# Norms spread over the update matmuls, four first units, a later convolution, and adaLN steps on ACT and POOL

## The chip, the cores and the metric

The kernel runs on one core of a Trainium2 chip. The time is that of one launch on the device, in microseconds (us); the lower the better. The engines are named as in the profile: PE does the matrix products and PEld loads their weights, DVE is the vector engine, ACT the activation engine, POOL the GpSimd engine, and SP starts most of the transfers (DMAs). Each engine works through its own list of instructions in order; it waits on semaphores for the others.

## The reference

The input is one sequence of 1024 tokens with 1024 channels and one conditioning vector c. Two layers follow each other; each has a mixer and a feed-forward part (ConvFFN), and each of these four blocks begins with a norm and ends with a gated addition to x. Cut to what matters here:

```
cs = silu(c)
for i in (0, 1):
    mod = cs @ ada_w[i] + ada_b[i]                 # (6 * 1024): the adaLN vector
    sh_m, sc_m, g_m, sh_f, sc_f, g_f = split(mod, 6)
    hm = rms_norm(x, norm_mix[i]) * (1 + sc_m) + sh_m
    y = even_mixer(hm) if i == 0 else odd_mixer(hm)
    x = x + g_m * y
    hf = rms_norm(x, norm_ffn[i]) * (1 + sc_f) + sh_f
    x = x + g_f * conv_ffn(hf)

conv_ffn(h): gate, val = split(h @ w_up, 2)        # 1024 -> 2 * 2816
    gate = causal_dwconv(gate, conv_w) + conv_b    # three taps over the tokens
    return (silu(gate) * val) @ w_down             # 2816 -> 1024
```

The even mixer is a gated delta rule beside windowed pooling, the odd one is dilated window attention with three groups of heads. All is float32.

## The kernel before

**Layout.** x lives as eight tiles `xt[k]` of 128 channels by 1024 tokens. Tokens are worked in two halves of 512 (`HS`). Every product is done three times (`mm3`, L203 to L208): each operand is split into a high part `hi` (rounded to the fast format) and a low part `lo` (the rest), and hi times hi, hi times lo and lo times hi are added up in PSUM. `split` (L182) makes a pair: ACT copies the high part (L183), another engine, POOL as a rule, subtracts it (L184). Weights come as granules of 128x512 numbers: a DMA into a `raw` tile (four of them in rotation), then `split` into `whi` and `wlo` (nine of each in rotation).

**PSUM.** There are two tiles `mm` (1024 columns) and four tiles `sp` (512 columns), each a rotation: who asks for the next one waits until the last reader of the oldest has finished.

**Order of the work.** The program is written as generators. A dense generator issues matmuls and yields the time of each step (`3 * MM`, 0.648 for an `mm3`); `weave` (L92) runs a chain of other work between them: where the chain yields a number, the dense generator is stepped until its yields add up to that number. When the kernel is built, a planner fixes the order of each engine's list from this text order and its own estimates of when each instruction is ready, so that a later instruction may stand ahead of an earlier one that is not yet ready. On the chip the lists run strictly in order.

**The edges.** Where one block ends and the next begins, the last four row blocks of the output product are added to x by half: `edge` (L423) issues the eight channel tiles of the first half, then `edge_end` (L417) weaves the norm of the first half into the matmuls of the second. Each finished tile is added to x by DVE (L240), squared by ACT (L343, L346), and the squares are summed by DVE (L347). `norm` (L384) sums over the channels with four PE transposes and a DVE reduction (L307, L308), takes the reciprocal root in twelve small DVE steps (`rsqrt`), spreads it into an `sp` tile by PE (L354), and then `normed` (L379) does for each of the eight tiles: DVE multiplies by the root, read from PSUM (L367), ACT applies scale and shift (L374), DVE makes the high part (L376), and the low part is subtracted by POOL for even tiles and by DVE for odd ones (L377). All eight tiles are issued in one go. There are three such edges: from the even mixer to its ConvFFN (about 530 us), from that ConvFFN to the odd mixer (about 1245 us), from the odd mixer to its ConvFFN (about 2365 us).

**The first units of ConvFFN.** `first_two` (L1138) computes the channel blocks 0 and 1 of gate and value. While the second half of h is not there, it runs three units over the first half (gate 0, value 0, gate 1), with the norm of the second half woven in; then gate 0, value 0 and gate 1 over the second half, and value 1 over both halves in a third `mm` tile. `conv_half` (L1109) does the convolution of one half out of PSUM: ACT the centre tap (L1102), DVE the others (L1098); `act` (L1119) applies silu and multiplies by the value. `h_sums` (L1172) and `w_sums` (L1227) then form sums of the blocks of h and of the weights, and the blocks 2 to 21 run as seven products each (`up`, L1232).

**The down stage.** For the 22 hidden blocks two at a time (a pair), `update` (L220) takes four granules and two hidden blocks (split into `oh` by ACT and `ol` by POOL, 128x1024 each), and does 16 units of two `mm3`; DVE adds each `sp` tile to x (L240).

**The adaLN steps.** The adaLN vector of the two layers is not computed at once: `ada_steps` (L260) does it in sections of 512 numbers with eight steps each. A step loads 128x512 weights into a `raw` tile and DVE multiplies them by a column of cs and adds them to `ada_acc` (L274 the first, L276 the others); after eight, PE and DVE sum over the partitions (`ada_cols`, L307, L308, L321). `step_back` (L109) issues one step at every second unit of the down stage of layer 0 (`pace[0] = 2`, L1274). The very first sections are done by `ada_pair` (L283), which can do a step on ACT and POOL: ACT scales the raw tile in place (L293), POOL adds it to the sum (L295).

## Time and profile before

| | us |
|---|---|
| median of 3 runs (lowest, highest) | 3082.81 (3079.80, 3086.07) |
| the profiled execution | 3081.34 |
| its span, first to last instruction | 3079.6 |

| engine | busy us | share of the span |
|---|---|---|
| PE | 2967.4 | 96% |
| DVE | 2018.0 | 66% |
| ACT | 1074.1 | 35% |
| POOL | 972.2 | 32% |

The span is the time from the first to the last instruction of the profiled execution; the launch has 1.7 us more. A busy share is an average over stages that differ; below, views of single stretches are shown, and the times in them are counted from the start of the span. `<-` after a wait names what ended it. PE is counted busy while a matmul's records say so; matmuls follow each other closer than their own durations, so that their spacing says more than their durations.

### The profile page before, as it was taken

Reading aid. Unit: us, or ns where it says so; the run is one execution under the profiler, and the core shown is the slowest. Engines: PE = TensorE matmul, PEld = TensorE weight load, DVE = VectorE, ACT = ScalarE, POOL = GpSimd, SP = SyncE. Lnnn points to the kernel's source line nnn. Section 1 sums busy time; section 2 is a strip of 40 time slices with the busy share of each in tenths; the row PEclk is TensorE's granted clock in tenths of the full one; section 3 lists DMA queues with packets and bytes.
Section 4 is the critical chain, followed back from the end, with each engine's and each line's share of the span. In section 5 each row is a group of like instructions: output and inputs, shape, how many; then the busy total and the mean of one; then the engine's idle time right before and its main releaser. Section 6 shows DMA issues by size and latency. Waiting matters only on the chain.

```text
span 3079.6 us, 40200 instructions
## 1 busy us (share of the span) xinstructions
PE 2967.4 (96%) x14346; PEld 2446.9 (79%) x14346; DVE 2018.0 (66%) x3877; ACT 1074.1 (35%) x2170; POOL 972.2 (32%) x727
## 2 busy tenths in 40 slices
PE   6999999899999899999999999999999899999999
PEld 4777878678888777788888878888877788888888
DVE  7877745987777877754445646354687877776554
ACT  4434422433333211323333333324343433333210
POOL 4412323555555543200000010000022655555540
PEclk8999999999999999999999999999999999999999
DMA  7523323253323753221313242313243222224321
GB/s 248 145 63 99 96 91 121 72 158 110 110 86 106 240 164 114 106 86 61 106 61 114 65 149 72 115 37 117 68 163 114 85 89 83 82 82 168 110 90 59
DMA packets 275010, 331.46 MB, mean 108 GB/s; under 512 B 27411, under 2 KB 194426, under 8 KB 274810
## 3 DMA queue, kind: packets, MB, share of 16 engines
q1 hardware_dynamic: 266810, 300.55, 31.0%
q0 software_dynamic: 7040, 25.17, 2.4%
q10 hardware_dynamic: 960, 3.18, 0.3%
q8 instruction: 113, 1.85, 0.2%
q14 instruction: 87, 0.71, 0.1%
HBM read 251.82 MB, written 77.00 MB: 107 GB/s over the span
## 4 chain that ended last, share of the span: by engine, by line
PE 72%; DVE 7%; DMA 3%; issue 2%; POOL 1%; ACT 1%; SPq 0%; POOLq 0%; DVEq 0%; ACTq 0%
PE sp L206 11%; PE sp L207 11%; PE sp L208 11%; PE mm L1356 8%; PE mm L1354 8%; PE mm L1355 8%; PE mm L206 3%; PE mm L207 3%; PE mm L208 3%; PE sp L1550 2%; PE sp L1506 2%; PE sp L1386 1%; DVE ada_acc L276 1%; PE sp L1539 1%; DMA raw<-in_ada_w_dram 1%
## 5 line engine op out<-in xcount | busy, mean ns | idle before, releaser
L1354 PE MATMUL mm<-whi,hh 128*128 128x512 f32 x1152 | 482.7, 419 | 0.0
L1356 PE MATMUL mm<-whi,hl 128*128 128x512 f32 x1152 | 452.7, 393 | 0.0
L1355 PE MATMUL mm<-wlo,hh 128*128 128x512 f32 x1152 | 451.6, 392 | 0.0
L184 POOL TENSOR_TENSOR wlo<-raw,whi 128x512 fp32r<-128x512 f32 x190 | 257.0, 1367 | 544.5 <-ACT whi L183 463.8
L183 ACT ACTIVATE whi<-raw 128x512 fp32r<-128x512 f32 x334 | 208.4, 630 | 389.6 <-PE sp L207 163.0
L240 DVE SCALAR_TENSOR_TENSOR xr<-sp,mod,xr 128x512 f32<-128x512 f32 x336 | 248.0, 747 | 135.6 <-PE sp L208 135.2
L206 PE MATMUL sp<-oh,whi 128*128 128x512 f32 (+1 forms) x832 | 315.6, 379 | 20.2 <-DVE xr L240 14.2
L207 PE MATMUL sp<-ol,whi 128*128 128x512 f32 (+1 forms) x832 | 311.1, 374 | 0.0
L208 PE MATMUL sp<-oh,wlo 128*128 128x512 f32 (+1 forms) x832 | 311.0, 374 | 0.0
L206 PE MATMUL mm<-hh,whi 128*128 128x512 f32 x736 | 299.6, 407 | 8.8 <-DVE ft L1098 6.8
L207 PE MATMUL mm<-hl,whi 128*128 128x512 f32 x736 | 294.0, 399 | 3.2 <-POOL hl L377 1.6
L208 PE MATMUL mm<-hh,wlo 128*128 128x512 f32 x736 | 293.1, 398 | 0.0
L184 POOL TENSOR_TENSOR wlo<-t2k,whi 128x512 fp32r<-128x512 f32 x160 | 228.8, 1443 | 159.0 <-ACT whi L183 120.7
L1451 POOL DMA_DIRECT2D vd<-v x24 | 17.6, 735 | 771.9 <-ACT v L1448 379.4
L1356 PEld LDWEIGHTS mm<-whi,hl 128*128 128x128 f32 x1152 | 216.6, 188 | 48.0
L1355 PEld LDWEIGHTS mm<-wlo,hh 128*128 128x128 f32 x1152 | 217.9, 189 | 37.2 <-DVE wlo L184 0.2
L1354 PEld LDWEIGHTS mm<-whi,hh 128*128 128x128 f32 x1152 | 217.5, 189 | 36.1
L184 POOL TENSOR_TENSOR wlo<-wr,whi 128x512 fp32r<-128x512 f32 x114 | 177.5, 1559 | 161.5 <-ACT whi L183 158.6
L206 PEld LDWEIGHTS sp<-oh,whi 128*128 128x128 f32 x832 | 157.0, 189 | 55.7 <-DVE xr L240 21.6
L208 PEld LDWEIGHTS sp<-oh,wlo 128*128 128x128 f32 x832 | 157.1, 189 | 28.2
L207 PEld LDWEIGHTS sp<-ol,whi 128*128 128x128 f32 x832 | 157.1, 189 | 26.3
L206 PEld LDWEIGHTS mm<-hh,whi 128*128 128x128 f32 x736 | 140.8, 191 | 38.8 <-issue 10.7
(395 smaller groups left out, 6147.4 us busy)
## 6 DMA issues: line engine op xcount, KB each, us to landing
raw<-in_ada_w_dram SPq DMA_DIRECT2D x160, 256.0 KB
wr<-in_ffn_w_up_dram SPq DMA_DIRECT2D x76, 512.0 KB
raw<-in_od_w_in_dram SPq DMA_DIRECT2D x144, 256.0 KB
hid<-ft SPq DMA_DIRECT2D x44, 512.0 KB
raw<-in_ffn_w_down_dram SPq DMA_DIRECT2D x88, 256.0 KB
big<-hid SPq DMA_DIRECT2D x44, 512.0 KB
xr<-xs SPq DMA_DIRECT2D x32, 512.0 KB
os<-stg SPq DMA_DIRECT2D x96, 130.0 KB
```

The source lines that it names most:

```text
L183: nc.scalar.activation(dst_hi, src, AF.Copy)
L184: eng.tensor_tensor(out=dst_lo, in0=src, in1=dst_hi, op=ALU.subtract)
L206: nc.tensor.matmul(ps, wh, mh, start=first, stop=False)
L207: nc.tensor.matmul(ps, wh, ml, start=False, stop=False)
L208: nc.tensor.matmul(ps, wl, mh, start=False, stop=last)
L240: nc.vector.scalar_tensor_tensor(out=xt[o][:, s], in0=p, scalar=gate[:, o:o + 1], in1=xt[o][:, s], op0=ALU.mult, op1=ALU.add)
L276: nc.vector.scalar_tensor_tensor(out=acc, in0=raw, scalar=cs[:, k:k + 1], in1=acc, op0=ALU.mult, op1=ALU.add)
L1354: nc.tensor.matmul(p, hh, wh, start=(k == 0), stop=False)
L1355: nc.tensor.matmul(p, hh, wl, start=False, stop=False)
L1356: nc.tensor.matmul(p, hl, wh, start=False, stop=(k == KT - 1))
L1506: nc.tensor.matmul(ps[:, at:at + len(ks) * P], qks[i][0][:, hh, blk * P:(blk + 1) * P], qks[i][1][:, hh, ks[0] * P:(blk + 1) * P], start=T ...
L1550: nc.tensor.matmul(ps[:, j * P:(j + 1) * P], pTs[n][:, a0 + c * P:a0 + (c + 1) * P], vb(kb, hh), start=(c == 0), stop=(c == len(ks) - 1))
```

## The change

The change has four parts.

1. In `norm`, the eight tiles are issued one at a time, with a yield of `apart` after each. `edge_end` sets `apart` to 1.3, so that steps of the update's second half stand between the tiles; the other callers leave it at zero. In `moved`, the high part of odd tiles is now made by ACT, straight from the tile before its scale and shift, ahead of the scale and shift in place; for even tiles DVE makes it as before.
2. In `first_two`, four units run over the first half (value 1 is the fourth, in an `sp` tile), and value 1 over the second half goes to a second `sp` tile; the third `mm` tile is no longer asked for. The second wait of the norm of the second half is 6.0 and no longer 5.5.
3. The convolution of the first half of gate 0 is issued after the matmuls of its second half, beside that of the second half.
4. From the down stage of layer 0 on, the adaLN steps run as in `ada_pair` on ACT and POOL: ACT scales the raw tile by the column of cs (in place, or into `ada_acc` for the first step), POOL adds it for the other seven.

```diff
--- before.py
+++ after.py
@@ -104,6 +104,7 @@
 
     pa = [None]
     back = []
+    by_pool = [False]
     beat, pace, secs_done, secs_due = [0], [3], [0], [12]
 
     def step_back(now=False):
@@ -270,7 +271,11 @@
             yield 1
             for k in range(KT):
                 nxt = load(s, k + 1) if k < KT - 1 else None
-                if k == 0:
+                if by_pool[0]:
+                    nc.scalar.activation(raw if k else acc, raw, AF.Copy, scale=cs[:, k:k + 1])
+                    if k:
+                        nc.gpsimd.tensor_tensor(out=acc, in0=acc, in1=raw, op=ALU.add)
+                elif k == 0:
                     nc.vector.tensor_scalar(out=acc, in0=raw, scalar1=cs[:, 0:1], scalar2=None, op0=ALU.mult)
                 else:
                     nc.vector.scalar_tensor_tensor(out=acc, in0=raw, scalar=cs[:, k:k + 1], in1=acc,
@@ -371,9 +376,12 @@
 
         a, b = vec
         s = HS[hf]
+        hh, hl = h[k]
+        if k % 2:
+            nc.scalar.activation(hh[:, s], t, AF.Identity, scale=a[:, k:k + 1], bias=b[:, k:k + 1])
         nc.scalar.activation(t, t, AF.Identity, scale=a[:, k:k + 1], bias=b[:, k:k + 1])
-        hh, hl = h[k]
-        nc.vector.tensor_copy(hh[:, s], t)
+        if not k % 2:
+            nc.vector.tensor_copy(hh[:, s], t)
         (nc.vector if k % 2 else nc.gpsimd).tensor_tensor(out=hl[:, s], in0=t, in1=hh[:, s], op=ALU.subtract)
 
     def normed(xt, vec, h, hf, rstd, ks=range(KT), keep=False):
@@ -381,11 +389,12 @@
         for k in ks:
             moved(scaled(xt, k, hf, rstd, keep), vec, h, k, hf)
 
-    def norm(xt, vec, h, hf, acc, wait=(2.5, 5.8), keep=False):
+    def norm(xt, vec, h, hf, acc, wait=(2.5, 5.8), keep=False, apart=0.0):
         yield wait[0]
         rstd = yield from rstd_row(acc[hf], wait[1])
-        normed(xt, vec, h, hf, rstd, keep=keep)
-        yield 1.2
+        for k in range(KT):
+            normed(xt, vec, h, hf, rstd, (k,), keep)
+            yield apart
 
     osp = dram.tile([8, P, T], F32, name="osp")
     osp2 = dram.tile([4, P, T], F32, name="osp2")
@@ -416,7 +425,7 @@
 
     def edge_end(acc, tl, xt, vec, h, keep=None):
 
-        weave(norm(xt, vec, h, 0, acc, keep=keep is not None), tl)
+        weave(norm(xt, vec, h, 0, acc, keep=keep is not None, apart=1.3), tl)
         drain(tl)
         return acc
 
@@ -1138,25 +1147,25 @@
             def first_two():
 
                 gp, vp = mm_ps(), mm_ps()
-                g = [[gp[:, s] for s in HS], [s_ps(), None]]
-                wb = [wu_gate(0), wu_val(0), wu_gate(1)]
+                g, v = ([[p[:, s] for s in HS], [s_ps(), None]] for p in (gp, vp))
+                wb = [wu_gate(0), wu_val(0), wu_gate(1), wu_val(1)]
                 t = [gate_tile(), gate_tile()]
-                d = units([gp, vp, g[1]], wb, h, (0,))
-                weave(norm(xt, vec, h, 1, acc, (4.5, 5.5), keep=True), d)
+                d = units([gp, vp, g[1], v[1]], wb, h, (0,))
+                weave(norm(xt, vec, h, 1, acc, (4.5, 6.0), keep=True), d)
                 drain(d)
-                conv_half(t[0], g[0], 0, 0)
                 drain(units([gp], wb[:1], h, (1,)))
-                conv_half(t[0], g[0], 0, 1)
+                for hf in range(2):
+                    conv_half(t[0], g[0], 0, hf)
                 conv_half(t[1], g[1], 1, 0)
                 drain(units([vp], wb[1:2], h, (1,)))
-                act(t[0], [vp[:, s] for s in HS], 0)
+                act(t[0], v[0], 0)
                 sums = h_sums()
                 g[1][1] = s_ps()
-                drain(units([[None, g[1][1]]], wb[2:], h, (1,)))
+                drain(units([[None, g[1][1]]], wb[2:3], h, (1,)))
                 conv_half(t[1], g[1], 1, 1)
-                vp = mm_ps()
-                drain(units([vp], [wu_val(1)], h))
-                act(t[1], [vp[:, s] for s in HS], 1)
+                v[1][1] = s_ps()
+                drain(units([[None, v[1][1]]], wb[3:], h, (1,)))
+                act(t[1], v[1], 1)
                 return sums
 
 
@@ -1271,7 +1280,7 @@
                 up(j, b, a)
                 a = nxt
             xt = reload(xs[2 + l])
-            pace[0] = 2
+            pace[0], by_pool[0] = 2, True
             for j in range(0, NJ - 4, 2):
                 if j:
                     hid = [from_dram(hid_d[l][i]) for i in (j, j + 1)]
```

## Rows read from the trace of the kernel before

**Rows 1.** Busy time by engine in stretches of 100 us: stretch, its length, then busy us (and instructions) of PE, PEld, DVE, ACT and POOL, the granted PE clock as a share of full speed, the DMA share and GB/s.
```profile
500.00:600.00 100.00, 89.63 (x392) 71.67 (x390) 75.71 (x123) 34.33 (x53) 41.78 (x27) 0.98 0.26 84
1000.00:1100.00 100.00, 90.70 (x386) 71.37 (x385) 80.09 (x100) 25.03 (x32) 51.41 (x29) 0.98 0.67 222
...
2900.00:3000.00 100.00, 100.00 (x443) 82.81 (x442) 55.21 (x74) 21.04 (x28) 44.19 (x27) 1.00 0.28 90
```

**Rows 2.** What PE waited for from 1000 to 1320 us (the down stage of layer 0 and the edge behind it): the PE instruction, what ended its wait, us in total, times, longest us.
```profile
PE sp L206 <- DVE xr L240: 14.2, 16, 2.4
PE sp L354 <- DVE rs L131: 1.2, 1, 1.2
PE sp L307 <- DVE t2k L347: 1.2, 1, 1.2
PE sp L206 <- DVE t2k L367: 1.1, 1, 1.1
```

**Rows 3.** The same from 500 to 640 us (the edge from the even mixer to its ConvFFN, and the first units).
```profile
PE mm L206 <- DVE ft L1098: 3.4, 1, 3.4
PE sp L206 <- DVE xr L367: 2.5, 1, 2.5
PE sp L307 <- DVE t2k L347: 2.1, 1, 2.1
PE sp L354 <- DVE rs L131: 1.3, 1, 1.3
PE mm L207 <- POOL hl L377: 0.9, 1, 0.9
PE mm L207 <- DVE hl L377: 0.8, 1, 0.8
```

**Rows 4.** PE's instructions in order of time at the edge from the odd mixer to its ConvFFN, those with a wait of over 2 us before them: start, us, line, operation, and in brackets the idle time before it and what ended it.
```profile
2382.98 0.47 PE L206 MATMUL sp<-oh,whi 128*128 128x512 f32 x1 [2.46 <-DVE xr L367]
...
2394.22 0.66 PE L307 MATMUL sp<-ident,t2k 128*128 128x128 f32 x4 [2.11 <-DVE t2k L347]
...
2432.85 0.71 PE L206 MATMUL mm<-hh,whi 128*128 128x512 f32 x1 [3.41 <-DVE ft L1098]
```

**Rows 5.** DVE's groups of instructions from 538.8 to 561.6 us, from the first tile of the norm of the first half to the last sum of squares of the second: line, operation, count, busy us, mean ns of one, idle us before them.
```profile
L376 DVE CAST hh<-xr 128x512 fp32r<-128x512 f32 x8 | 6.4, 794 | 0.0
L347 DVE TENSOR_TENSOR t2k<-t2k,t2k 128x512 f32<-128x512 f32 x6 | 6.0, 1002 | 0.2
L367 DVE TENSOR_TENSOR xr<-xr,sp 128x512 f32<-128x512 f32 x8 | 5.3, 676 | 0.8 <-PE sp L354 0.8
L240 DVE SCALAR_TENSOR_TENSOR xr<-sp,mod,xr 128x512 f32<-128x512 f32 x5 | 3.6, 738 | 0.0
L377 DVE TENSOR_TENSOR hl<-xr,hh 128x512 fp32r<-128x512 f32 x4 | 3.2, 804 | 0.0
```

**Rows 6.** ACT's groups in the same stretch.
```profile
L374 ACT ACTIVATE xr<-xr,mod,nA 128x512 f32<-128x512 f32 x8 | 6.4, 811 | 3.9 <-DVE xr L367 3.9
L183 ACT ACTIVATE whi<-raw 128x512 fp32r<-128x512 f32 x7 | 4.2, 621 | 0.4 <-issue 0.4
L346 ACT ACTIVATE t2k<-xr 128x512 f32<-128x512 f32 x6 | 3.7, 630 | 2.6 <-DVE xr L240 2.5
```

**Rows 7.** DVE's instructions in order of time, at two places: columns as in rows 4.
```profile
558.32 3.20 DVE L347 TENSOR_TENSOR t2k<-t2k,t2k 128x512 f32<-128x512 f32 x2
565.93 0.69 DVE L1227 TENSOR_TENSOR t2k<-raw,raw 128x512 f32<-128x512 f32 x1 [4.41 <-DMA raw<-in_ffn_w_up_dram]
566.54 0.68 DVE L308 TENSOR_REDUCE rs<-sp 128x4 f32<-128x512 f32 x1
...
1037.50 0.82 DVE L274 TENSOR_SCALAR ada_acc<-raw,cs 128x512 f32<-128x512 f32 x1
```

**Rows 8.** PE's instructions in order of time, at two places: the first and last of seven matmuls after the wait that ended at 561.58 us, the first after them, and the transposes of an adaLN section.
```profile
562.65 0.63 PE L206 MATMUL sp<-hh,whi 128*128 128x512 f32 x1
...
565.21 0.63 PE L206 MATMUL mm<-hh,whi 128*128 128x512 f32 x1
...
566.19 0.40 PE L206 MATMUL sp<-hh,whi 128*128 128x512 f32 x1
...
1063.02 0.60 PE L307 MATMUL sp<-ident,ada_acc 128*128 128x128 f32 x4
```

**Rows 9.** Groups of instructions from 1020 to 1215 us, the down stage of layer 0 (columns as in rows 5).
```profile
L240 DVE SCALAR_TENSOR_TENSOR xr<-sp,mod,xr 128x512 f32<-128x512 f32 x130 | 94.3, 744 | 25.7 <-PE sp L208 25.4
L276 DVE SCALAR_TENSOR_TENSOR ada_acc<-raw,cs,ada_acc 128x512 f32<-128x512 f32 x48 | 57.8, 1205 | 12.5 <-DMA raw<-in_ada_w_dram 12.3
L184 POOL TENSOR_TENSOR wlo<-raw,whi 128x512 fp32r<-128x512 f32 x36 | 49.2, 1379 | 48.0 <-ACT whi L183 35.2 <-PE sp L208 6.4 <-PE sp L207 6.3
...
L184 POOL TENSOR_TENSOR ol<-big,oh 128x1024 fp32r<-128x1024 f32 x18 | 44.7, 2487 | 51.3 <-PE sp L207 29.7 <-ACT oh L183 19.7 <-PE sp L208 1.9
```

**Rows 10.** One of POOL's groups from 0 to 110 us, where `ada_pair` does its steps on ACT and POOL (columns as in rows 5).
```profile
L295 POOL TENSOR_TENSOR ada_acc<-ada_acc,whi 128x512 f32<-128x512 f32 x3 | 4.2, 1397 | 2.7 <-ACT whi L293 2.6
```

**Rows 11.** Who waited for whom from 1015 to 1215 us, all engines: three of the rows (columns as in rows 2).
```profile
ACT whi L183 <- PE sp L207: 52.0, 8, 10.1
...
POOL ol L184 <- PE sp L207: 29.7, 5, 8.4
...
DVE ada_acc L276 <- DMA raw<-in_ada_w_dram: 13.7, 8, 3.2
```

## The prediction

> **What bounds the kernel now.** I read the busy time in stretches of 100 us first [rows 1]. From 2900 to 3000 us PE runs 443 instructions in 100 us and never idles: there the matmuls alone set the time, 0.226 us each and 0.68 for an `mm3`. The stretches that the change touches fall short of that, 392 instructions from 500 us and 386 from 1000 us, with DVE at 76 and 80 us of 100. So the kernel is bound by PE, and time is to be won only where PE waits. The waits say where that is, and each of them names DVE or what DVE feeds. In the down stage of layer 0 it is 14.2 us in 16 waits for the gated addition L240, which frees an `sp` tile [rows 2]. At the edge into layer 0's ConvFFN it is 3.4 + 2.5 + 2.1 + 1.3 + 0.9 + 0.8 = 11.0 us [rows 3], at the same edge of layer 1 three of these come again with the same length [rows 4], and I take the edges as equal, and at the edge between the layers 1.2 + 1.2 + 1.1 = 3.5 us [rows 2]. A wait costs more than itself: behind the one that ended at 561.58 us, PE was at the lower of its two levels, seven matmuls from 562.65 us spaced by (565.21 - 562.65) / 6 = 0.43 us, which is 512 columns at 1.2 GHz, against 0.23 us after 566.19 us [rows 8]. That is 7 x 0.2 = 1.4 us, and I take as much behind the 3.4 us wait: 2.6 us of clock for an edge. All in all 14.2 + 2 (clock) + 2 x 13.6 + 3.5 = 47 us can be won at most, as far as these rows reach.
>
> **Part 4, the down stage.** Why is L240 late? It takes 744 ns each time, so nothing slows it; but in DVE's list it stands behind L276, 48 steps of a mean 1205 ns with 12.5 us of idle before them for the weights' DMA [rows 9]. A step has the form of L240 but reads both inputs from SBUF, as POOL's subtractions do; L240 reads one from PSUM, and keeps its 744 ns beside a POOL that is busy half the time. I read the 0.46 us that a step takes longer as time lost against POOL, and take it that more work on POOL will not lengthen L240.
>
> With the change DVE keeps L240 alone, 94 us of 200. All 14.2 us of waits and the clock behind the first, 2 us, go, and bounds are 0 and 16 us by these rows. The work goes to ACT, 54 scalings of about 0.63 us (the nearest row is a square of the same size, 630 ns [rows 6]) = 34 us on an engine with 25 us busy of 100 [rows 1], and to POOL, 48 additions of 1.40 us, the row of the same addition at the start [rows 10], = 67 us. POOL has 49.2 + 44.7 = 94 us already [rows 9], so 161 us of some 183 us: 88%, the fullest engine after PE. What it delays is `wlo` and `ol`, which stand behind additions that wait for ACT, and ACT for the DMA (13.7 us for DVE now [rows 11]). The cover is their lead: ACT waits 52.0 us and POOL 29.7 us for PE to give tiles back [rows 11], so they are done about a pair ahead, and PE waits for neither in the whole stage [rows 2]. The transposes of an adaLN section sit in PE's list too; those at 1063.02 us [rows 8] belong to a section whose eight steps were over when the next began at 1037.50 us [rows 7], 25 us earlier, so POOL may be that late. The cover is thin only in the first two pairs, where hidden blocks and weights come in while the steps start. There I leave 2 us, and take a gain of 14 us.
>
> **Parts 1 to 3, an edge into a ConvFFN.** I go along the waits.
>
> The 2.5 us: PE wants an `sp` tile while the root's tile is held by all eight multiplications (L367) and the additions L240 stand behind them. Tile by tile, 1.3 lets pass three `mm3` (0.648 each, two are short of it), so the additions stand between the tiles. The root's tile stays held longer, until the last tile, but three others rotate at 12 x 0.226 = 2.7 us each. This wait goes; the work behind it does not. From 538.8 to 561.6 us DVE never idles, but for 1.0 us at its start [rows 5]. Of its 22.8 us the change takes four of the eight casts, 6.4 / 2 = 3.2 us, which leaves 19.6. From the same start PE has 19 `mm3` of the update and 7 before the transposes, 26 x 0.68 = 17.7 us. So the transposes still wait about 2 us (now 2.5 + 2.1). ACT gets four more, 4 x 0.81, and one more granule: 14.3 + 3.2 + 0.6 = 18.1 us [rows 6], also beside 17.7, so it is no cover for DVE but not behind it. Bounds of this remainder: 0 and 4.6 us.
>
> The 1.3 us: the reduction L308 stands behind a sum of weights L1227 that waited 4.41 us for its DMA [rows 7]. The raw tiles of value 1 now stand ahead of those sums in the rotation, so this DMA starts later in the text's order, while the update that frees `whi` ends earlier. The wait of the root has one `mm3` more of cover (10 for 6.0, 9 for 5.5). I take 0.7 us, bounds 0 and 4.4.
>
> The 0.9 + 0.8 us for `hl` of the second half: a fourth unit of 8 x 0.68 = 5.4 us stands before the first use, against a lack of under a microsecond each. Gone.
>
> The 3.4 us: value 1 waited for the `mm` tile of gate 0, which frees after the convolution L1098. With two `sp` tiles that question is gone, and the later convolution is covered by the four units of the second half, 21.8 us. What is late next: all four `sp` tiles are then held by gate 1 and value 1, and block 2's second product needs one, which frees after the convolution of gate 1, behind the same DVE work. Bounds 0 and 3.4; I take 1.0.
>
> New: the fourth unit needs two more granules in the first round, and the nine `whi` are held by the update until its end; 0 to 1.5 us by ACT's 0.62 and POOL's 1.4 for one [rows 6, 9], taken 0.7. For the clock I leave 0.7 of 2.6.
>
> Sum of what stays: 2 + 0.7 + 1.0 + 0.7 + 0.7 = 5.1 of 13.6, a gain of 8.5 us, twice: 17. The edge between the layers has no first units; there the same casts go and the 1.1 us wait for a tile, and I take 2 of 3.5.
>
> **Sum.** 14 + 17 + 2 = 33 us. The profiled execution took 3081.3 us (span 3079.6 and 1.7 around it), so 3048.3; the median of the runs is 1.5 us above that execution, which gives 3049.8. I say 3049.
>
> **Rivals.** First, the edges only move their waits: DVE and ACT have 19.6 and 18.1 us of work for 17.7 us of PE, and every handoff from ACT to DVE within a tile can stall both lists. For it speaks that PE's waits at the edges are all for DVE's chain; against it, that 3.4 + 1.7 us of them hang on tiles and order that the change alters. Then only the down stage gains: 3082.8 - 14 - 1 = 3068.
>
> Second, the down stage gains nothing, because the four raw tiles are now held for DMA, ACT and POOL in a row, and the steps and the granules share them. Against it speaks the lead of a pair. Then 3082.8 - 19 = 3064.
>
> Third, slower: POOL becomes the bound of the down stage. Per pair it has 4 x 1.379 + 2 x 2.487 = 10.5 us and 48 / 9 = 5.3 additions. PE needs 22.2 us a pair (96 matmuls of 0.226 and the transposes), so up to (22.2 - 10.5) / 5.3 = 2.2 us for an addition, its waiting in POOL's list included, nothing happens. The kernel is slower by 6 us, the edges' gains included, when nine pairs take 14.2 + 2 + 19 + 6 = 41 us beyond PE's need, 4.6 each: 3.1 us an addition, 1.7 of it waiting. Then 3089 and more. DVE's steps waited 13.7 / 48 = 0.3 us each on the DMA [rows 11], so I hold it unlikely. The Trainium skill, GPSIMD Engine Reference, section "4.1 Engine selection", speaks for this rival: it gives elementwise additions to VectorE and calls GPSIMD about twice as slow; 1397 against 744 ns agrees, and by the rule alone 48 x 0.65 = 31 us of engine time are lost, which on the path, beside the edges' gain, would give 3081.3 + 31 - 19 = 3093.
>
> Fourth, no effect: the planner's order makes new waits of the size of those that go, say a root delayed by 4.4 us or more at each edge and the slow first pairs; then within 6 us of 3082.8.
>
> **Chances.** The forecast, 3038 to 3060: 0.60. All waits gone, 3030 to 3037: 0.04. Edges only moved: 0.13. Down stage without gain: 0.11. No effect: 0.05. Slower: 0.07. A measurement of this kernel tells about 0.2%, 6.2 us, from no change. So faster 0.88, the same 0.05, slower 0.07. The range takes in the two half gains: 3032 to 3070; the forecast's own is 3038 to 3060.
>
> **What would show it.** In the down stage, PE's waits for L240 are gone, DVE is at some 94 us of 200, POOL near 160, and PE waits neither for `wlo`, `ol` nor for the transposes of a section; waits for POOL there would prove the third rival. At the edges, no wait for L367 and none for `hl`, none for an `mm` tile behind L1098, and one of about 2 us for L347. If that one is 4 us or more, the first rival is right. A DMA wait ahead of L308 longer than 4.4 us would show the order wrong. More than 6 us at the start of block 2 would break the fourth term of the edge.

## The result, and the profile after

The changed kernel takes 3064.0 us (median of 6 runs, 3061.65 to 3069.38), the kernel before 3085.0 beside it: a ratio of 0.9935 [0.9922, 0.9948]. On the 3082.8 us of the prediction that is 20 us less, where 33 were forecast; the range of 3032 to 3070 holds it. The profiled execution had a span of 3067.3 us, the longest of the six.

Both traces have 14346 matmuls, and PE runs them in nearly the same order. So the start of the k-th matmul can be set beside that of the same matmul before, and the offset tells where time is won and lost (worked out from the traces' PE records; the last column is from a second trace of the changed kernel, which is told of under the experiments):

| k-th matmul | starts before (us) | offset after (us) | what lies since the row above | gained (-) or lost | the same, second trace |
|---|---|---|---|---|---|
| 200 | 74.4 | +3.1 | start and first norm | +3.1 | +4.2 |
| 2400 | 504.4 | +3.1 | even mixer | 0.0 | -1.9 |
| 3000 | 657.8 | +0.6 | edge into ConvFFN 0 | -2.5 | -2.4 |
| 5400 | 1218.4 | -20.6 | up stage and down stage | -21.2 | -21.1 |
| 5700 | 1287.7 | -14.0 | end of the down stage, edge between the layers | +6.6 | +5.2 |
| 11000 | 2351.5 | -12.8 | odd mixer | +1.2 | -2.4 |
| 11500 | 2478.3 | -12.2 | edge into ConvFFN 1 | +0.6 | 0.0 |
| 14346 | 3074.8 | -12.2 | ConvFFN 1 | 0.0 | 0.0 |

Nearly all that is won is won in the down stage, a quarter to a third of that is lost right behind it, the two edges into a ConvFFN give 1.9 and 2.4 us together, and the start loses 2 to 4. In the mixers, which the change leaves alone, the two traces of one kernel differ by 1.9 and 3.6 us. So a row is read only where several traces agree on it.

Even the 2.5 us of the first edge are not the edit's. Up to matmul 2960, at 645 us, the changed kernel has lost 0.6 us there. What it wins, 3.1 us from #2960 to #3000, lies behind the end of [rows 3], at a wait that is 2.05 us in the kernel before and 0.6 in the changed one:

```profile
650.26 0.47 PE L206 MATMUL sp<-t,whi 128*128 128x512 f32 x1 [2.05 <-DVE ft L1244]
```

A kernel whose edge is that of the kernel before (part 4 alone, below) has only 0.4 us of this wait and wins 3.2 us there too.

The busy time of the changed kernel by stretches of 100 us (columns as in [rows 1]):

```profile
1000.00:1100.00 100.00, 100.00 (x449) 82.80 (x448) 60.46 (x83) 43.23 (x58) 77.05 (x51) 1.00 0.66 209
1100.00:1200.00 100.00, 100.00 (x452) 82.45 (x450) 61.71 (x82) 38.11 (x54) 74.57 (x51) 1.00 0.53 158
1200.00:1300.00 100.00, 94.07 (x407) 75.32 (x406) 58.58 (x112) 44.00 (x65) 24.67 (x24) 0.97 0.35 118
```

Up to 1200 us the down stage now looks like the stretch that PE alone bounds: 100.00 us busy, 449 matmuls where [rows 1] had 386. The next 100 us fall back to 94 and a granted clock of 0.97. The groups of the changed kernel from 1000 to 1200 us (columns as in [rows 9]):

```profile
L241 DVE SCALAR_TENSOR_TENSOR xr<-sp,mod,xr 128x512 f32<-128x512 f32 x144 | 107.4, 750 | 77.6 <-PE sp L209 77.6
...
L277 POOL TENSOR_TENSOR ada_acc<-ada_acc,raw 128x512 f32<-128x512 f32 x49 | 63.6, 1299 | 20.0 <-ACT ada_acc L275 12.0 <-ACT raw L275 6.1 <-POOL ada_acc L277 0.2
L185 POOL TENSOR_TENSOR ol<-big,oh 128x1024 fp32r<-128x1024 f32 x20 | 48.0, 2401 | 12.7 <-ACT oh L184 12.5
L185 POOL TENSOR_TENSOR wlo<-raw,whi 128x512 fp32r<-128x512 f32 x33 | 42.2, 1293 | 17.0 <-ACT whi L184 17.0
```

This answers to [rows 9]: L241 (L240 before) keeps its length, 750 against 744 ns, and what it waits for is PE, 77.6 us. POOL has 63.6 + 48.0 + 42.2 = 153.8 of 200 us, and its idle time was spent waiting for ACT. PE's waits at the places of [rows 2 to 4], one fence each. From 1000 to 1320 us (columns as in [rows 2]):

```profile
PE sp L209 <- POOL wlo L185: 1.9, 2, 1.2
PE sp L207 <- ACT whi L184: 1.6, 2, 1.0
PE sp L312 <- DVE t2k L352: 1.1, 1, 1.1
PE sp L359 <- DVE rs L132: 1.1, 1, 1.1
```

From 500 to 640 us, the first edge, all that PE waited for:

```profile
PE sp L207 <- DVE ft L1107: 6.5, 1, 6.5
PE sp L209 <- POOL wlo L185: 2.5, 1, 2.5
PE sp L207 <- ACT whi L184: 1.7, 1, 1.7
```

From 2300 to 2480 us, the third edge:

```profile
PE sp L207 <- DVE ft L1107: 3.7, 1, 3.7
...
PE sp L209 <- POOL wlo L185: 2.5, 1, 2.5
PE sp L207 <- DVE ft L1253: 2.3, 1, 2.3
PE sp L207 <- ACT whi L184: 1.6, 1, 1.6
```

The 16 waits for L240 are gone, and so are all six of [rows 3]. At the first edge 10.7 us of others stand in the place of 11.0: the granules of the first round (`whi`, `wlo`: 4.2) and an `sp` tile that the convolution L1107 (L1098 before) gives back late (6.5).

### The profile page after: what moved, and what is told of

The parts are those of the page before. It is cut to its first block, busy times and chain, and to the rows that moved or that the text cites. A ratio compares the mean times of both kernels' runs of the same rounds, so it can differ in the third digit from the quotient of the medians.

```text
span 3067.3 us, 40298 instructions
## 1 busy us (share of the span) xinstructions
PE 2965.9 (97%) x14346; PEld 2452.8 (80%) x14346; DVE 1945.1 (63%) x3781; ACT 1138.9 (37%) x2266; POOL 1033.0 (34%) x783
## 4 chain that ended last, share of the span: by engine, by line
PE 73%; DVE 6%; POOL 2%; issue 2%; DMA 2%; ACT 1%; SPq 0%; POOLq 0%; ACTq 0%; DVEq 0%
PE sp L209 11%; PE sp L207 11%; PE sp L208 11%; PE mm L1365 8%; PE mm L1363 8%; PE mm L1364 8%; PE mm L208 3%; PE mm L207 3%; PE mm L209 3%; PE sp L1559 2%; PE sp L1515 2%; PE sp L1395 1%; DVE xr L1181 1%; PE sp L1548 1%; POOL wlo L185 1%
## 5 line engine op out<-in xcount | busy, mean ns | idle before, releaser
L185 POOL TENSOR_TENSOR wlo<-raw,whi 128x512 fp32r<-128x512 f32 x190 | 250.0, 1331 | 492.6 <-ACT whi L184 425.0
L241 DVE SCALAR_TENSOR_TENSOR xr<-sp,mod,xr 128x512 f32<-128x512 f32 x336 | 251.1, 749 | 183.5 <-PE sp L209 183.5
L207 PE MATMUL mm<-hh,whi 128*128 128x512 f32 x704 | 285.3, 405 | 1.7 <-DVE big L609 1.7
L208 PE MATMUL mm<-hl,whi 128*128 128x512 f32 x704 | 280.0, 398 | 2.2 <-DVE hl L385 2.2
L209 PE MATMUL mm<-hh,wlo 128*128 128x512 f32 x704 | 279.8, 397 | 0.0
L207 PE MATMUL sp<-hh,whi 128*128 128x512 f32 x384 | 152.3, 396 | 13.5 <-DVE ft L1107 10.2
```

Source lines behind the costliest of these rows:

```text
L185: eng.tensor_tensor(out=dst_lo, in0=src, in1=dst_hi, op=ALU.subtract)
L207: nc.tensor.matmul(ps, wh, mh, start=first, stop=False)
L208: nc.tensor.matmul(ps, wh, ml, start=False, stop=False)
L209: nc.tensor.matmul(ps, wl, mh, start=False, stop=last)
L241: nc.vector.scalar_tensor_tensor(out=xt[o][:, s], in0=p, scalar=gate[:, o:o + 1], in1=xt[o][:, s], op0=ALU.mult, op1=ALU.add)
```

## The experiments

Twelve kernels ran. They come from the changed kernel by the edits shown, but for the first, which comes from the kernel before.

**Which part pays.** Part 4 alone, on the kernel before:

```diff
+                if by_pool[0]:
+                    nc.scalar.activation(raw if k else acc, raw, AF.Copy, scale=cs[:, k:k + 1])
+                    if k:
+                        nc.gpsimd.tensor_tensor(out=acc, in0=acc, in1=raw, op=ALU.add)
...
-            pace[0] = 2
+            pace[0], by_pool[0] = 2, True
```

> The kernel before with part 4 alone. Theory: part 4 wins some 21 us in the down stage and gives 6 to 7 back right behind it, where the last eight weight granules wait behind adaLN tiles in the rotation of four; so about 15 us faster than before, ratio 0.995, and PE waits for whi and wlo in the last update although the edge is the old one. Rival: that loss belongs to the new norm at the edge (ACT's copies, spread tiles); then this kernel has no such waits and is 20 us or more faster, ratio 0.9935 or less.

Measured: 0.9955 [0.994, 0.997]. That is what was expected. By the k-th matmul it wins 21.0 us from #3000 to #5400 and loses 7.8 from there to #5700, as the whole change does, with waits of 2.3 us for `wlo` and 1.4 for `whi` beside the old edge. The loss belongs to part 4. All but part 4:

```diff
-            pace[0], by_pool[0] = 2, True
+            pace[0] = 2
```

> The changed kernel without part 4, so parts 1 to 3 alone. Theory: they are worth next to nothing together (some 2.5 us won at the first edge, 0 at the third, 2 to 3 lost at the start, where the same function makes the first h): ratio 0.998 to 1.001, with PE waiting at each edge into a ConvFFN about 4 us for the fourth unit's granules and 4 to 6.5 us for an sp tile at block 2. Rival: parts 1 to 3 bring 6 us or more (ratio 0.998 or less), and the rest of what the changed kernel lacks was lost by part 4.

Measured: 0.9976 [0.9964, 0.9988]; the down stage is as before (0.0 us, and 14.5 us of waits for L241 are back), nothing is lost behind it, and edge 2 wins 1.7. Parts 1 to 3 are worth about 0.24%, 7 us [4, 11] (2.8 by the last matmul of the profiled execution), not 19. So the ratio agrees with the rival (6 us or more) and the trace with the theory, and the interval leaves both; that the loss is part 4's holds either way. The two ratios give 0.45 + 0.24 = 0.69% together, and the change 0.65%: as far as the intervals tell, the parts add up and neither hides the other.

**What is lost behind the down stage.** SP's list of the changed kernel near the end of the stage (start, us from the first issue to the last, line, transfer, count):

```profile
1170.47 22.84 SPq L265 DMA_DIRECT2D raw<-in_ada_w_dram  x11
1194.37 10.04 SPq L189 DMA_DIRECT2D raw<-in_ffn_w_down_dram  x8
```

Eleven adaLN tiles go through the four raw tiles before the last eight granules of `w_down` may: what is left of the steps is issued ahead of the last block (`sections(24)`, L1292). They take 22.84 us, and the granules start at 1194. The same order, no faster, stands in the kernel before:

```profile
1166.55 23.45 SPq L264 DMA_DIRECT2D raw<-in_ada_w_dram  x11
1191.03 10.72 SPq L188 DMA_DIRECT2D raw<-in_ffn_w_down_dram  x8
```

So the eleven loads are not slower with ACT and POOL than they were with DVE; why they take that long in both is not shown here. What has changed is when PE asks: the matmul that waits first, at 1202.88 us in the changed kernel, began at 1221.39 before, and the last granules are issued 2.7 us later than they were. The loads did not follow when PE won 21 us, and a delay that the waits for L240 had covered came out. PE's instructions there, those with a wait, and two of those behind them (columns as in [rows 4]):

```profile
1202.88 0.50 PE L209 MATMUL sp<-oh,wlo 128*128 128x512 f32 x1 [1.22 <-POOL wlo L185]
...
1203.92 0.50 PE L207 MATMUL sp<-oh,whi 128*128 128x512 f32 x1 [0.54 <-ACT whi L184]
...
1205.34 0.50 PE L209 MATMUL sp<-oh,wlo 128*128 128x512 f32 x1 [0.69 <-POOL wlo L185]
...
1206.88 0.80 PE L207 MATMUL sp<-oh,whi 128*128 128x512 f32 x1 [1.04 <-ACT whi L184]
...
1208.82 0.63 PE L207 MATMUL sp<-oh,whi 128*128 128x512 f32 x1
1209.25 0.63 PE L208 MATMUL sp<-ol,whi 128*128 128x512 f32 x1
```

The waits are 3.5 us; behind them the spacing is 1209.25 - 1208.82 = 0.43 us, the lower of the two levels of the clock. Two cures that have nothing in common tell whether it is the shared rotation: the steps of the stage in tiles of their own,

```diff
-                back.append(ada_steps(1, range(0, 48, 4), raw_tile))
+                back.append(ada_steps(1, range(0, 48, 4), lambda: t2k() if by_pool[0] else raw_tile()))
```

> The changed kernel, with the adaLN weights of the down stage loaded into the t2k rotation of eight (idle there) and no longer into the raw rotation of four that the granules use. Theory: the 6 to 8 us lost right behind the down stage come from the last eight granules, which wait for raw tiles behind eleven adaLN tiles; with tiles of their own PE has no whi or wlo wait there and the kernel is 6 us faster than the changed one, ratio about 0.9915. Rival: POOL or ACT themselves are late (161 us of work in 183); then the granules come as late as before, within 1.5 us of the changed kernel.

and more steps in the up stage, so that fewer are left for the down stage:

```diff
-                secs_due[0], pace[0] = 24, 14
+                secs_due[0], pace[0] = 24, 10
```

> The changed kernel with a step every 10 products, not every 14, in the up stage of layer 0, so that some 16 of the steps run there on DVE and the down stage has fewer. Theory: the steps end before the last granules are due; the 6 to 8 us behind the down stage go, the up stage stays bound by PE (DVE at 75 us of 100): ratio about 0.9915. Rival: the up stage's DVE has no room and the up stage grows by what the edge wins; within 2 us of the changed kernel.

Measured: 0.9913 [0.9895, 0.9931] and 0.9902 [0.9887, 0.9917]. Both theories hold. From #5400 to #5700 they win 1.7 and 1.3 us on the kernel before, where the changed kernel loses 6.6. The gain from #3000 to #5400 is 21.7 us with pace 10 and 18.5 with tiles of their own: there PE waits 2.4 us for POOL's `ol` once, at 1018 us, in the first pairs, which no kernel with the shared rotation does. (Their ratios hold more than this: they also win 7.3 and 7.0 us at the first edge, which the cures don't touch; the last section has the reason.) SP's list with tiles of their own:

```profile
1159.08 20.33 SPq L189 DMA_DIRECT2D raw<-in_ffn_w_down_dram  x8
```

The last granules of `w_down` are issued by 1159.08 + 20.33 = 1179.4 us and not by 1194.37 + 10.04 = 1204.4. With pace 10, all of PE's waits from 1000 to 1290 us:

```profile
PE sp L312 <- DVE t2k L352: 1.1, 1, 1.1
PE sp L359 <- DVE rs L132: 1.1, 1, 1.1
```

No `whi` and no `wlo`. The loss of 8 us (6.6 + 1.7, or 1.3) comes from the adaLN loads that stand ahead of the last granules in the one rotation.

**The edges.** Part 2 undone, parts 1, 3 and 4 kept:

```diff
-                wb = [wu_gate(0), wu_val(0), wu_gate(1), wu_val(1)]
+                wb = [wu_gate(0), wu_val(0), wu_gate(1)]
...
-                d = units([gp, vp, g[1], v[1]], wb, h, (0,))
-                weave(norm(xt, vec, h, 1, acc, (4.5, 6.0), keep=True), d)
+                d = units([gp, vp, g[1]], wb, h, (0,))
+                weave(norm(xt, vec, h, 1, acc, (4.5, 5.5), keep=True), d)
...
-                v[1][1] = s_ps()
-                drain(units([[None, v[1][1]]], wb[3:], h, (1,)))
-                act(t[1], v[1], 1)
+                vp = mm_ps()
+                drain(units([vp], [wu_val(1)], h))
+                act(t[1], [vp[:, s] for s in HS], 1)
```

> The changed kernel with three first units again (part 2 undone; parts 1, 3 and 4 kept). Theory: the fourth unit costs more than it covers: without it the granule waits of 1.7 + 2.5 us and the sp wait of 6.5 and 3.7 us go from both edges, the 3.4 us wait for an mm tile comes back, and the kernel is 5 to 10 us faster than the changed one, ratio about 0.991 to the one before. Rival: the sp wait is DVE's backlog and only changes its name; then the mm wait is as long as the sp wait was (4 to 6 us), and the kernel is within 3 us of the changed one.

Measured: 0.9925 [0.991, 0.994], 3 to 4 us faster than the changed kernel by ratio and median, which lies between the theory and the rival and inside both intervals; the profiled third edge wins 7.1 us where the changed kernel loses 0.6 (the first: 3.6 and 2.5). The granules' waits and that for the `sp` tile are gone. PE's waits of this kernel from 500 to 640 us:

```profile
PE mm L208 <- DVE hl L385: 3.0, 3, 1.2
PE sp L312 <- DVE t2k L352: 3.0, 1, 3.0
PE mm L207 <- DVE ft L1132: 2.3, 1, 2.3
PE sp L359 <- DVE rs L132: 1.5, 1, 1.5
PE mm L207 <- DVE ft L1107: 0.3, 1, 0.3
```

10.1 us of waits again: against [rows 3] the one for L1107 (3.4 before) is 0.3, with part 3 in place, those for L352 and `hl` are longer, and one of 2.3 us for the `mm` tile that L1132 frees is new. The casts back on DVE, everything else as changed:

```diff
-        if k % 2:
-            nc.scalar.activation(hh[:, s], t, AF.Identity, scale=a[:, k:k + 1], bias=b[:, k:k + 1])
         nc.scalar.activation(t, t, AF.Identity, scale=a[:, k:k + 1], bias=b[:, k:k + 1])
-        if not k % 2:
-            nc.vector.tensor_copy(hh[:, s], t)
+        nc.vector.tensor_copy(hh[:, s], t)
```

> The changed kernel with all high parts made by DVE again (that half of part 1 undone). Theory: the 2.2 us wait for hl near 66 us of the span and with it 2 to 3 us at the start go, and at the edges DVE has 3.2 us more and ACT 3.2 us less work each, so that the granule waits (ACT's splits come earlier) shrink while the waits for DVE grow: within 3 us of the changed kernel. Rival: ACT's copies relieve the edges; then this kernel is 5 us or more slower than the changed one.

Measured: 0.993 [0.9915, 0.9945], within 3 us of the changed kernel, as expected. At the edges the copies on ACT mostly move the waits: with all casts on DVE, PE waits 3.1 us for L352 again, and 1.1 for the granules in place of 4.2. At the start they cost 2.9 us (+0.2 against +3.1 at #200): `moved` also serves the first norm, where ACT is what PE's first products wait for. ACT in the changed kernel there, and the wait that comes of it, which the kernel before does not have:

```profile
62.35 1.53 ACT L382 ACTIVATE t2k<-t2k,mod,nA 128x512 f32<-128x512 f32 x2 [4.19 <-DVE nA L549]
63.78 0.80 ACT L381 ACTIVATE hh<-t2k,mod,nA 128x512 fp32r<-128x512 f32 x1
64.49 1.51 ACT L382 ACTIVATE t2k<-t2k,mod,nA 128x512 f32<-128x512 f32 x2
```
```profile
68.87 0.56 PE L208 MATMUL mm<-hl,whi 128*128 128x512 f32 x1 [2.16 <-DVE hl L385]
```

ACT does 0.71 us more for every second tile. At #200 the seven kernels that have ACT's copies from the start on are 2.7 to 4.2 us late, the six that have none there 0.1 to 1.9, this one 0.2. Three units, and ACT's copies from the first edge on only:

```diff
-        if k % 2:
+        if k % 2 and on_act[0]:
...
-        if not k % 2:
+        if not (k % 2 and on_act[0]):
...
+        on_act[0] = True
         weave(norm(xt, vec, h, 0, acc, keep=keep is not None, apart=1.3), tl)
```

> Three first units again, and ACT makes the odd high parts only from the first edge on, DVE at the start. Theory: the start is back to that of the kernel before (3 us less than the changed kernel by the 200th PE instruction), and the edges are those of the kernel with three units: about 3 us faster than that one, ratio 0.9915. Rival: the 3 us at the start are noise of the first loads; then the 200th instruction is as late as in the changed kernel.

The same three units with all casts on DVE (the edits of both):

> Three first units and all high parts by DVE: of the changes to the edges only the spread tiles and the later convolution are left. Theory: ACT's copies are worth 1 to 3 us at each edge into a ConvFFN with three units, so this is 2 to 5 us slower than the kernel with copies at the edges only. Rival: the copies bring nothing, because ACT is as full as DVE there; then the two agree within 1.5 us.

Measured: 0.9897 [0.9882, 0.9912] and 0.9918 [0.9901, 0.9935], 3052.3 against 3059.6 us. Between the two that is 7.3 us, where 2 to 5 were expected, and the first is some 8 us faster than the kernel with three units above, where 3 were. At #200 it is 1.4 us late and that one 3.6, so the loss at the start comes with the copies. With three units the copies on ACT are worth 3.0 us at the first edge (5.3 against 2.3 by the k-th matmul) and 5.0 at the third (6.9 against 1.9); PE's wait for L352 is 3.0 us with them and 5.3 without, at both. All tiles issued in one go again:

```diff
-        weave(norm(xt, vec, h, 0, acc, keep=keep is not None, apart=1.3), tl)
+        weave(norm(xt, vec, h, 0, acc, keep=keep is not None), tl)
```

> The changed kernel with the eight tiles of the first half's norm issued in one go again (apart 0; all else as changed). Theory: the spread tiles won the 2.5 us wait for an sp tile and brought the sums of squares forward; without them PE waits for the root's tile (DVE L372) again at the edges, 2 to 3 us each, and the kernel is 4 to 8 us slower than the changed one. Rival: the granules of the fourth unit are what the edge waits for anyway, so the wait for the sp tile hides inside; within 2 us of the changed kernel.

Measured: 0.9906 [0.989, 0.9923], 7 us faster than the changed kernel beside it, the opposite of what was expected; the first edge wins 10.5 us in place of 2.5, the third 5.2. PE's waits of this kernel from 520 to 640 us:

```profile
PE sp L207 <- DVE ft L1107: 2.1, 1, 2.1
...
PE sp L209 <- POOL wlo L185: 1.3, 1, 1.3
PE sp L207 <- DVE xr L372: 0.7, 1, 0.7
```

The wait for the root's tile, which the spreading was to remove, is 0.7 us without it (2.5 in [rows 3]). ACT's splits of the next weights, without spreading and in the changed kernel, one fence each:

```profile
552.24 1.66 ACT L184 ACTIVATE whi<-raw 128x512 fp32r<-128x512 f32 x3
```
```profile
553.63 0.62 ACT L184 ACTIVATE whi<-raw 128x512 fp32r<-128x512 f32 x1
...
557.84 1.14 ACT L184 ACTIVATE whi<-raw 128x512 fp32r<-128x512 f32 x2
```

With the tiles spread, the second and third of the four splits stand 5.1 us later, behind tiles of the norm; 1.8 us of that is the whole trace, which is later by as much (it spreads the root at 540.80 us, the other at 538.99). PE's first round waits for them.

The start of block 2 (#2800 at the first edge, #11320 at the third) lies ahead of the wait for L1107, and parts the edges in two. Offsets gained (-) or lost against the kernel before, worked out as in the first table:

| kernel | first edge, #2400 to #2800 | #2800 to #2960 | third edge, #11000 to #11320 | #11320 to #11500 |
|---|---|---|---|---|
| changed | -8.8 | +9.4 | -9.1 | +9.7 |
| changed, second trace | -9.8 | +10.2 | -9.7 | +9.8 |
| without part 4 | -9.8 | +9.2 | -9.8 | +9.9 |
| adaLN tiles of their own | -9.8 | +6.4 | -9.7 | +6.4 |
| pace 10 | -8.9 | +4.7 | -8.9 | +6.7 |
| all tiles in one go | -11.9 | +4.3 | -11.6 | +6.4 |
| all casts on DVE | -7.8 | +9.8 | -7.8 | +8.7 |
| three units | -6.8 | +2.6 | -7.8 | +0.7 |
| part 4 alone (edge as before) | +1.7 | 0.0 | -0.1 | 0.0 |

Up to block 2, where all the waits of [rows 3] lie, the changed kernel wins 9 to 10 us an edge, and behind it gives all of it back. Three units win less and lose much less. Without the spreading they win some 2 to 3 us more up to block 2, at both edges and against each of the five other traces with ACT's copies and four units. So the spreading costs that much an edge. Behind block 2 the kernel without it loses as little as the two cures above, in which the tiles are spread, so the rest of its 7 us is not the spreading's; it belongs to the last section.

**Is the long wait for L1107 chance?** The changed kernel once more, unaltered:

> The changed kernel once more, for its trace. The wait at block 2 (DVE L1107) was 6.5 and 3.7 us in its first trace, and 2.1 and 0.4 us in kernels whose DVE list is the same there; in these, eight subtractions L1181 ran in a row while POOL waited, and there DVE and POOL took turns. Theory: which of the two happens is left to the moment, and a second trace of the same kernel may show the other; then some 2 to 5 us of each edge are spread between executions and not the edit's. Rival: it is fixed by the program; then this trace has 6.5 and 3.7 us again.

Measured: 0.9934 [0.9915, 0.9954], and the waits for L1107 are 6.5 and 3.7 us again, as the rival has it. The kernel without part 4 has 6.5 and 3.7 us as well. Two traces of one kernel are few, but they speak for the program and against the moment.

**The best together.** Three units, ACT's copies from the first edge on, and the adaLN steps in tiles of their own, or pace 10:

> Three first units, ACT's copies from the first edge on, and the adaLN weights of the down stage in the t2k rotation: the three findings together. Theory: stage by stage they add up; against the kernel with three units and copies from the first edge on, the 7 us behind the down stage go, so 3045 to 3049 us, ratio 0.988. Rival: what is won there is lost to the next wait; then no faster than 3051.

> The same with the raw rotation as it was and a step every 10 products in the up stage of layer 0, the other cure of the late granules. Theory: the same gain, 3045 to 3049 us. Rival: with three units the up stage's DVE is fuller and takes 2 us or more of it back.

Measured: 0.9886 [0.987, 0.9902] and 0.9867 [0.9852, 0.9883]. The second takes 3044.9 us, 39 less than the kernel before beside it and 19 less than the changed one, as forecast. The first takes 3051.3 and misses its 3045 to 3049; PE's wait for `ol` is there again, 2.2 us. Their intervals overlap. Waits of 2 to 3 us for L352 and for `hl` stay at the second's edges. Three units without the spreading were not tried.

## Why the prediction was right, and where it was not

**The down stage: right, undersized in the middle and wrong at its end.** Waits for L240 gone, DVE left with that line (107.4 of 200 us; the 94 forecast stood for 130 additions, and 144 pass now), POOL near 160 (153.8): each step is as written. 14 us of waits plus 2 of clock were to be had at most; 21.2 came. The shortfall in matmuls was the better size: [rows 1] had 386 in the first of the two stretches and the row below 417 in the second, where 449 and 452 now pass, and (449 + 452 - 386 - 417) x 0.226 = 22 us.

```profile
1100.00:1200.00 100.00, 95.09 (x417) 76.42 (x416) 82.22 (x104) 18.66 (x25) 44.26 (x25) 1.00 0.53 160
```

The difference is in the restarts. One of the 16 waits of [rows 2], and the start behind it:

```profile
1043.71 0.50 PE L206 MATMUL sp<-oh,whi 128*128 128x512 f32 x1 [0.87 <-DVE xr L240]
1044.05 0.39 PE L207 MATMUL sp<-ol,whi 128*128 128x512 f32 x1
```

A wait is counted from the end of the last matmul's record (0.39 us long, where the starts are 0.227 us apart), which lies some 0.16 us behind the place where the next start would have been, and the start behind the wait comes after 0.34 us in place of 0.227. Over the 900 starts from #4500 to #5400 before, the spacing beyond 0.227 us is 17.0 us at the waits, 2.5 at other slow starts (those just behind a wait, for the most part) and 1.6 at eight starts of the lower clock: 21.1 us, for 14.2 us of listed waits.

The step that failed is "The cover is thin only in the first two pairs": PE waited for nothing there. It was thin in the last, and 2 us had been left for what cost 8. The working counted what ACT and POOL have to do, and gave them a lead of a pair; it did not ask whether the loads would keep up with a PE that is 21 us earlier, behind eleven adaLN tiles in the raw rotation. The second rival named the shared rotation and priced it at the whole stage. The sharing cost something at the end only, as the two cures show; that the tiles are held longer, the rival's other half, is not what the loads show (22.84 us against 23.45). That 14 us forecast stand against 21 - 8 = 13 measured is luck: two misses cancel. POOL's share was misread besides: its 161 us belong to nine pairs, which by the prediction's own 22.2 us take PE 200 us and not 183, so 80% and not 88; measured were 77%. The cover in the first pairs was indeed thin where adaLN has tiles of its own (the 2.4 us for `ol`).

**The third rival** did not come: an addition took 1299 ns, with the idle time before it (63.6 + 20.0) / 49 = 1.7 us, where the bound was 2.2 us, and from 1000 to 1200 us PE waits for nothing of POOL's. By the Trainium skill, GPSIMD Engine Reference, "4.1 Engine selection", an elementwise addition belongs on VectorE, and GPSIMD is about twice as slow at one with two inputs. The trace is near that length, 1299 ns against the 750 of DVE's addition from PSUM, and does not bear out the choice here: 49 slower additions on POOL, off DVE's list, won 21 us, because DVE's steps stood in front of what PE waits for.

**The edges: wrong in size, 17 us forecast, 1.9 measured** (and 7 for parts 1 to 3 by the run without part 4, edge 2 included). One term makes nearly all of the miss. Without its 1.0 us for block 2, the working has 13.6 - 2 - 0.7 - 0.7 - 0.7 = 9.5 us won an edge, and up to block 2 the changed kernel won 8.8 to 9.8 in two traces; its terms up to there miss by as much as 3.5 us and cancel, so this sum is luck in part. The step that failed is "I take 1.0" for the `sp` tile at block 2: 9.4 to 10.2 us are lost from there on. By its terms:

- The 2.5 us and both waits for `hl`: gone, as forecast. But the first owes little to the reason given, the three `mm3` between the tiles: without them it is 0.7 and 1.0 at the two edges.
- "The transposes still wait about 2 us" for L347: none at either edge, but only because PE has waited 4.2 us for granules just before. In the kernel with three units, which has no such waits, it is 3.0. The reduction behind it waits for PE now and for no DMA, which a wait longer than 4.4 us there would have contradicted.
- The granules of the fourth unit: taken 0.7, bound 1.5; measured 2.5 + 1.7 = 4.2 at the first edge and 2.5 + 1.6 at the third. The working priced one granule of ACT and POOL, and left out that the splits have a place in ACT's list, behind the tiles that are issued between updates.
- "I take 1.0" for the next `sp` tile at block 2, bound 3.4: 6.5 and 3.7. The mechanism was named, its size was not. What the waits don't show is the clock behind them (the next item) and a second wait for the same backlog, for the `sp` tile that L1253 frees: none at the first edge in one trace, 0.8 in the other, and 2.3 at the third. It is the test that the prediction set itself ("more than 6 us at the start of block 2").
- Clock: 0.7 left of 2.6. Behind the 6.5 us wait alone it is more:

```profile
616.25 0.77 PE L207 MATMUL sp<-hh,whi 128*128 128x512 f32 x1 [6.49 <-DVE ft L1107]
...
621.51 0.63 PE L207 MATMUL sp<-ext,whi 128*128 128x512 f32 x1
```

These are thirteen starts, at the end 0.43 us apart: 621.51 - 616.25 - 12 x 0.227 = 2.5 us on top of the wait.

So it was the first rival, "the edges only move their waits", that came true at the edges, with 0.13; its price for the whole, 3068, is 4 us from the result. The second rival's 3064 meets the result by chance alone: it gave the gain to the edges and none to the down stage. The forecast's own range of 3038 to 3060 does not hold the time; the wide one does.

**The edge between the layers:** 2 us forecast, 1.7 by the run without part 4.

**Left out altogether:** the first norm. The change to `moved` was worked through at the edges, and its other caller was not looked up: 2 to 4 us.

## What to carry to other kernels

Before a helper is changed, list its callers: `moved` paid at the edges and cost 2 to 4 us at the start. When a stage gets faster, ask whether its loads get faster with it: two streams in one rotation of tiles run in one order, and a delay that PE's waits had covered comes out, here at the end of the stage, behind eleven loads that took as long before. Of a wait that goes, ask which backlog it was: the same DVE work stood behind four tiles in place of two, and a wait of 3.4 us became one of 6.5. And size what a stage can win by its missing matmuls, not by its listed waits: 14.2 us of waits were 21 us of time.

## What was not expected of the hardware

DVE's and POOL's lists at the first edge are in the same order in the changed kernel and in the one with pace 10, and yet they pass differently. DVE in the changed kernel, and POOL beside it (columns as in [rows 4]):

```profile
592.59 0.68 DVE L1181 TENSOR_TENSOR xr<-xr 128x512 f32<-128x512 f32 x1
593.20 1.78 DVE L1181 TENSOR_TENSOR xr<-xr,xr 128x512 f32<-128x512 f32 x1
```
```profile
589.29 1.63 POOL L185 TENSOR_TENSOR wlo<-raw,whi 128x512 fp32r<-128x512 f32 x1 [3.68 <-ACT whi L184]
592.81 1.61 POOL L185 TENSOR_TENSOR ext<-xr,ext 128x512 fp32r<-128x512 f32 x1 [1.89 <-ACT ext L184]
```

And DVE and POOL with pace 10:

```profile
592.19 0.68 DVE L1181 TENSOR_TENSOR xr<-xr,xr 128x512 f32<-128x512 f32 x1
```
```profile
589.38 5.86 POOL L185 TENSOR_TENSOR wlo<-raw,whi 128x512 fp32r<-128x512 f32 x1 [3.68 <-ACT whi L184]
```

In the one, the engines take turns, and a subtraction of 0.68 us becomes one of 1.78. In the other DVE runs on, and one subtraction of POOL's takes 5.86 us in place of 1.3. DVE is then done with the same list at 594.0 in place of 598.3, and PE waits 2.1 us for L1107 and not 6.5. The Trainium skill, SBUF — State Buffer, "SBUF: two separate sides", says that the two engines share a pair of ports that, when DVE reads two inputs from SBUF and POOL reads SBUF too, one of them holds for a whole instruction while the other stands still; 0.68 against 1.78 us and the 5.86 agree with that. Which of the two comes next when both stand ready is what decides 4.4 us here, and no run shows what sets it: in both kernels POOL's instruction begins 0.2 us into a subtraction of DVE's (589.29 - 589.10 and 589.38 - 589.18), the changed kernel took turns both times that it was profiled, as did the one without part 4, and DVE ran on in the two cures and in the kernel without spreading (5.85 to 5.86 us for POOL's instruction). In each of these six traces the third edge goes as the first did, so it is not decided anew each time. Nor is it the order: the lists of DVE, ACT and POOL in the kernel with adaLN tiles of its own are, by line and tile, those of the changed kernel up to 980 us, and it still goes the other way. By the k-th matmul the difference between pace 10 and the changed kernel is 7.0 - 2.5 = 4.5 us at the first edge and 2.1 + 0.6 = 2.7 at the third. It is less than the wait for L1107 at the third edge would say (3.7 against 0.4), because part of it comes back as the wait for L1253 (2.3 against 4.2). So some 7 us of the time of the changed kernel hang on something that stays open, and the forecast did not know of it.
